# Every inverse norm of a hybrid decoder layer as one power on GpSimd, in place of a shift and three Newton steps on VectorE

## The chip, the cores and the metric

The kernel runs on one core of a Trainium2 chip. The metric is device time in microseconds (us), as the median of several executions. The core has five engines that run their own instruction queues in order: TensorE (PE, with its weight loads shown as PEld), VectorE (DVE), ScalarE (ACT), GpSimd (POOL) and SyncE (SP, which issues the DMAs here). An instruction that waits for a semaphore holds up all that stands behind it in the queue of its own engine.

## The reference, cut to what matters

The layer is: RMS norm of the input, one wide projection, two mixers (sparse attention, and a gated linear recurrence, HGRN2), an output projection with residual, a second RMS norm and a SwiGLU FFN. What the change touches is every place where a mean of squares is turned into its inverse root:

```
def rms_norm(x, g):
    y = xf * lax.rsqrt(jnp.mean(xf * xf, axis=-1, keepdims=True) + RMS_EPS)
    return y * g
h  = rms_norm(x, norm_mix[l])                      # 1024 tokens
q  = rms_norm(q.reshape(B, T, H, dh), q_norm[l])   # 8 heads a token
kc = rms_norm(compress(kc_raw, ...), k_norm[l, 0]) # 63 compressed keys, 2 groups
ks, kw = rms_norm(ks, ...), rms_norm(kw, ...)      # 2 groups a token each
o  = rms_norm(o, o_gain) * silu(hg)                # 4 HGRN heads
h  = rms_norm(x, norm_ffn[l])                      # 1024 tokens again
```

## The kernel before, in words

Tokens lie on the 128 partitions, in NT = 8 tiles of 128. Matmuls of full precision are made of three passes of split operands (lines 118 to 120, "mm3"): ACT writes the high part of an operand (line 111 or 114) and DVE the rest (line 112 or 115). The kernel is written in program order, and a scheduler in the tile framework sorts the instructions into the queue of each engine, so that the place of one in its queue can change when others are added or removed.

The stages, with the span's microseconds: the projection's first two blocks (0 to 80), in which the squares of the input rows are summed on ACT (line 262) and rsx, one inverse norm for each of 8 token tiles, is made (line 264); four HGRN heads (80 to 270), each with seven levels of a recurrence and then an output norm o_rs (lines 417 to 430); the queries, the compressed keys (norm rs), the norm rs_q of all queries (128 x 64) and four batches of keys (norm k_rs, lines 637 to 651) up to 395; the attention units from 395 to 740, with tiles of the output projection between them; a passage to the FFN (740 to 776); and the FFN to the end.

The function rsqrt (line 122) is called 19 times: once for rsx, four times for o_rs, once each for rs and rs_q, four times for k_rs, and eight times for n_rs, in norm_stats (line 239). Each call is v = mean + eps (line 125, a tile named rs_v), a shift (126), a subtraction from a constant (127), and three times a square, a product and a step (129, 130, 131), all on DVE: twelve instructions.

What follows a norm: in an HGRN head o_rs is multiplied by rsx (line 421), scales the head's output out of PSUM (424), which is gated (426) and transposed by PE (429); next stand on PE the first products of the next head (358). In the keys' stage k_rs scales kraw (647), then gain, cast and rest (648 to 650), and PE transposes (657). In the attention stage nsa_out (line 733) sums the squares of a finished token tile on ACT (242), takes n_rs, scales the tile on ACT (745), and multiplies by the gain on POOL (746) for tiles 0 to 6; tile 7 is scaled by one DVE instruction (743). POOL scales each head's weights in the same stage (850), with values that PE then transposes (861). In the passage PE transposes tiles and differences of tiles (724), and ACT and DVE write them as split operands (727, 728); POOL makes two of the differences of a tile (988, 989).

Of the kernel before, what the change touches and what calls it, by code (L numbers as in the profile page):

```python
# [8 lines left out]
F32 = mybir.dt.float32  # L9
F32R = mybir.dt.float32r  # L10
BF16 = mybir.dt.bfloat16
I32 = mybir.dt.int32
U8 = mybir.dt.uint8
AF = mybir.ActivationFunctionType
OP = mybir.AluOpType
# [3 lines left out]
P = 128  # L19
# [29 lines left out]
def hybrid_layer(ctx: ExitStack, tc: tile.TileContext, x, x_t, par, w_in, k_norm, pos_k, pos_v,  # L49
                 ck_w1, ck_w2, cv_w1, cv_w2, w_out, norm_ffn, w_gu, w_down, cst, hmask, out):  # L50
    nc = tc.nc
    V, A, G, PE = nc.vector, nc.scalar, nc.gpsimd, nc.tensor

    const = ctx.enter_context(tc.tile_pool(name="const", bufs=1))
    small = ctx.enter_context(tc.tile_pool(name="small", bufs=2))
# [65 lines left out]

    def rsqrt(y, ss, n, scale, eps, parts=P):
        v = small.tile([P, 64], F32, name="rs_v", tag="rs_v")[:parts, :n]
        t = small.tile([P, 64], F32, name="rs_t", tag="rs_t")[:parts, :n]
        V.tensor_scalar(v, ss, scale, eps, op0=OP.mult, op1=OP.add)
        V.tensor_scalar(t.bitcast(I32), v.bitcast(I32), 1, None, op0=OP.logical_shift_right)
        V.tensor_scalar(y.bitcast(I32), t.bitcast(I32), -1, 0x5F3759DF, op0=OP.mult, op1=OP.add)
        for _ in range(3):
            V.tensor_tensor(t, y, y, op=OP.mult)
            V.scalar_tensor_tensor(t, t, -0.5, v, op0=OP.mult, op1=OP.mult)  # L130
            V.scalar_tensor_tensor(y, t, 1.5, y, op0=OP.add, op1=OP.mult)


    ident = const.tile([P, P], F32, name="ident")
    make_identity(nc, ident)
    identb = const.tile([P, P], BF16, name="identb")
    V.tensor_copy(identb, ident)
    par_t = const.tile([P, 18], F32, name="par_t")
    gains = const.tile([P, 24], F32, name="gains")
    lb_a = const.tile([P, 4], F32, name="lb_a")  # L140
# [98 lines left out]
    def norm_stats(src, junk):  # L239
        ss = small.tile([P, 1], F32, name="n_ss", tag="n_ss")  # L240
        rs = small.tile([P, 1], F32, name="n_rs", tag="n_rs", bufs=NT)
        A.activation(junk, src, AF.Square, accum_out=ss)
        rsqrt(rs, ss, 1, 1.0 / D, EPS)
        return rs
# [5 lines left out]
    with tc.tile_pool(name="p0", bufs=1) as p0:  # L250
# [8 lines left out]
        def x_stats(t):  # L259
            xn = p0.tile([P, D], F32, name="xn", tag="xn", bufs=2)  # L260
            nc.sync.dma_start(xn, x[0, t * P:(t + 1) * P, :])
            A.activation(xn, xn, AF.Square, accum_out=ssx[:, t:t + 1])
            if t == NT - 1:
                rsqrt(rsx, ssx, NT, 1.0 / D, EPS)
                V.tensor_scalar(rsh, rsx, 0.5, None, op0=OP.mult)
# [85 lines left out]
    def hgrn_head(h, hp, fp, qp, kp):  # L351
# [65 lines left out]
        for k in range(2):  # L417
            A.activation(kp[:, 512 * k:512 * (k + 1)], so[k], AF.Square)
        V.tensor_reduce(ss, kp.rearrange("p (c t) -> p c t", c=NT), axis=AX.X, op=OP.add)
        rsqrt(rs, ss, NT, 1.0 / P, 4 * EPS)  # L420
        V.tensor_tensor(rs, rs, rsx, op=OP.mult)
        for k in range(2):
# [875 lines left out]
```

## Time and profile before

| what | us |
|---|---|
| median of 3 executions | 1403.97 (1402.77 to 1405.27) |
| profiled execution | 1403.17 |
| span of its instructions | 1401.3 |
| PE busy | 1369.5 (98%) |
| DVE busy | 1049.3 (75%), 1893 instructions |
| ACT busy | 596.0 (43%) |
| POOL busy | 393.8 (28%), 341 instructions |

The profile gives one execution. Busy time of PE contains the latency of pipelined matmuls, so that a busy PE may still have gaps of some tenths of a microsecond. In a timeline a row gives start and length in us, the engine, the line, what it writes and reads, and in brackets the idle time before it with what ended that. The granted clock of PE was 0.996 of full speed over the span.

### The profile page before, as it was taken

Reading aid. Unit: us, or ns where it says so; the run is one execution under the profiler, and the core shown is the slowest. Engines: PE = TensorE matmul, PEld = TensorE weight load, DVE = VectorE, ACT = ScalarE, POOL = GpSimd, SP = SyncE. Lnnn points to the kernel's source line nnn. Section 1 sums busy time; section 2 is a strip of 40 time slices with the busy share of each in tenths; the row PEclk is TensorE's granted clock in tenths of the full one; section 3 lists DMA queues with packets and bytes.
Section 4 is the critical chain, followed back from the end, with each engine's and each line's share of the span. In section 5 each row is a group of like instructions: output and inputs, shape, how many; then the busy total and the mean of one; then the engine's idle time right before and its main releaser. Section 6 shows DMA issues by size and latency. Waiting matters only on the chain.

```text
span 1401.3 us, 19716 instructions
## 1 busy us (share of the span) xinstructions
PE 1369.5 (98%) x7092; PEld 1129.2 (81%) x7092; DVE 1049.3 (75%) x1893; ACT 596.0 (43%) x1153; POOL 393.8 (28%) x341
## 2 busy tenths in 40 slices
PE   9999999999999999999998999999999999999998
PEld 7888888989977777787776888888888888887787
DVE  5317888626688888789877888888888887589864
ACT  7323333323447666566664433333333333444332
POOL 0001111011045442443436433233232230158500
PEclk9999999999999999999999999999999999999999
DMA  9411110111220001000003333333333328987431
GB/s 336 116 45 31 31 31 28 54 31 46 89 93 1 1 1 61 31 16 31 16 23 98 95 102 97 113 98 113 113 107 99 111 98 285 330 308 270 162 107 54
DMA packets 108769, 135.72 MB, mean 97 GB/s; under 512 B 6112, under 2 KB 63872, under 8 KB 108672
## 3 DMA queue, kind: packets, MB, share of 16 engines
q1 hardware_dynamic: 108672, 134.46, 28.7%
q8 instruction: 56, 0.92, 0.3%
q14 instruction: 41, 0.34, 0.1%
HBM read 105.87 MB, written 28.57 MB: 96 GB/s over the span
## 4 chain that ended last, share of the span: by engine, by line
PE 83%; DVE 12%; ACT 2%; issue 2%; POOL 1%; ACTq 0%; POOLq 0%; DVEq 0%
PE bank L118 9%; PE bank L119 9%; PE bank L120 9%; PE a L118 8%; PE a L119 8%; PE a L120 8%; PE ps_t L119 4%; PE ps_t L118 4%; PE ps_t L120 4%; PE ps_t L861 3%; DVE wop L112 2%; PE a L865 2%; PE a L866 2%; PE ps_t L375 1%; PE ps_s L839 1%
## 5 line engine op out<-in xcount | busy, mean ns | idle before, releaser
L850 POOL TENSOR_SCALAR pbig<-pbig,den,gates 128x640 f32<-128x640 f32 (+7 forms) x128 | 103.5, 812 | 165.5 <-DVE den L849 145.6
L111 ACT ACTIVATE wop<-rpage 128x512 fp32r<-128x512 f32 x132 | 82.7, 630 | 157.8 <-PE bank L120 70.7
L112 DVE TENSOR_TENSOR wop<-rpage,wop 128x512 fp32r<-128x512 f32 x132 | 101.0, 767 | 14.8 <-ACT wop L111 12.6
L864 DVE TENSOR_TENSOR ph<-ps_t,ph 128x512 fp32r<-128x512 f32 x126 | 84.4, 684 | 18.4 <-ACT ph L863 17.4
L863 ACT ACTIVATE ph<-ps_t 128x512 fp32r<-128x512 f32 x126 | 72.6, 595 | 48.2 <-PE ps_t L861 38.5
L381 POOL TENSOR_TENSOR kp<-kp,fp 128x256 f32<-128x256 f32 x28 | 20.3, 724 | 232.3 <-PE bank L358 180.7
L861 PE MATMUL ps_t<-ident,pbig 128*128 128x128 f32 x504 | 78.4, 275 | 2.1 <-POOL pbig L850 2.1
L112 DVE TENSOR_TENSOR wop<-act_a,wop 128x512 fp32r<-128x512 f32 x48 | 47.6, 991 | 32.0 <-ACT wop L111 31.9
L1012 POOL TENSOR_TENSOR tmp<-tmp,rpage 128x512 f32<-128x512 f32 x21 | 31.2, 1487 | 138.9 <-DVE wop L112 138.9
L861 PEld LDWEIGHTS ps_t<-ident,pbig 128*128 128x128 f32 x504 | 60.8, 141 | 11.7 <-POOL pbig L850 3.2
L112 DVE TENSOR_TENSOR wlo<-wraw,whi 128x1024 fp32r<-128x1024 f32 (+2 forms) x27 | 32.0, 1188 | 46.0 <-PE a L120 19.3
L848 ACT ACTIVATE pbig<-ps_s,nm 128x640 f32<-128x640 f32 (+3 forms) x64 | 55.9, 875 | 24.1 <-DVE nm L847 19.0
L119 PE MATMUL bank<-wop 128*128 128x512 f32 x165 | 65.0, 394 | 0.0
L120 PE MATMUL bank<-wop 128*128 128x512 f32 x165 | 64.9, 393 | 0.0
L111 ACT ACTIVATE wop<-act_a 128x512 fp32r<-128x512 f32 x48 | 30.3, 631 | 81.2 <-PE bank L120 56.4
L118 PE MATMUL bank<-wop 128*128 128x512 f32 x165 | 64.8, 393 | 0.0
L847 DVE TENSOR_REDUCE nm<-ps_s 128x1 f32<-128x640 f32 (+3 forms) x64 | 58.1, 914 | 4.7 <-PE ps_s L842 3.1
L865 PE MATMUL a<-ph,kv 128*128 128x512 f32 x132 | 58.6, 444 | 2.1 <-ACT ph L863 1.3
L866 PE MATMUL a<-ph,kv 128*128 128x512 f32 x132 | 57.3, 434 | 2.8 <-DVE ph L864 2.3
L972 POOL TENSOR_TENSOR tmp<-rpage 128x512 f32<-128x512 f32 x20 | 27.4, 1369 | 115.7 <-DMA rpage<-in_w_gate_up_dram 115.7
L112 DVE TENSOR_TENSOR wop<-tmp,wop 128x512 fp32r<-128x512 f32 x42 | 43.6, 1039 | 20.6 <-ACT wop L111 19.2
L111 ACT ACTIVATE wop<-tmp 128x512 fp32r<-128x512 f32 x42 | 26.6, 633 | 70.2 <-POOL tmp L1012 37.5
(458 smaller groups left out, 4454.5 us busy)
## 6 DMA issues: line engine op xcount, KB each, us to landing
rpage<-in_w_gate_up_dram SPq DMA_DIRECT2D x86, 256.0 KB, 3.1
raws<-in_w_down_dram SPq DMA_DIRECT2D x35, 512.0 KB, 7.2
act_a<-act_d SPq DMA_DIRECT2D x12, 1024.0 KB, 6.2
act_d<-as SPq DMA_DIRECT2D x33, 256.0 KB, 2.2
act_e<-act_d SPq DMA_DIRECT2D x6, 1024.0 KB, 7.6
act_d<-tmp SPq DMA_DIRECT2D x22, 256.0 KB, 2.2
act_d<-th SPq DMA_DIRECT2D x22, 256.0 KB, 2.1
xn<-in_x_dram SPq DMA_DIRECT2D x8, 512.0 KB, 5.5
```

Of the source, the lines that this page charges most:

```text
L111: A.activation(hi, src, AF.Copy)
L112: V.tensor_tensor(lo, src, hi.bitcast(F32), op=OP.subtract)
L118: PE.matmul(o, ah, bh, start=first, stop=False, skip_group_check=chained)
L119: PE.matmul(o, ah, bl, start=False, stop=False, skip_group_check=chained)
L120: PE.matmul(o, al, bh, start=False, stop=last, skip_group_check=chained)
L847: V.tensor_reduce(nm, sv, axis=AX.XY, op=OP.max, negate=True)
L850: G.tensor_scalar(pp, pp, den, gates[:, qb, h * 3 + 1 + b:h * 3 + 2 + b], op0=OP.mult, op1=OP.mult)
L861: PE.transpose(pt[:, r * P:(r + 1) * P], wts[r][:, c0:c0 + P], ident)
L863: A.activation(ph[:, 0], pt, AF.Copy)
L864: V.tensor_tensor(ph[:, 1], pt, ph[:, 0].bitcast(F32), op=OP.subtract)
L865: PE.matmul(o, vst[b][:, kb, g, :], ph[:, 0], start=b == 0 and kb == kb0, stop=False)
L866: PE.matmul(o, vst[b][:, kb, g, :], ph[:, 1], start=False, stop=False)
```

## The change

The shift, the subtraction and the nine Newton instructions of rsqrt are gone; v stays on DVE, and one GpSimd instruction raises it to the power -0.5, elementwise, with a constant tile of -0.5 as its second operand. That tile is set once, by a DVE memset at the program's start. Lines behind this function carry numbers that are lower by four after the change (421 becomes 417).

```
     def rsqrt(y, ss, n, scale, eps, parts=P):
         v = small.tile([P, 64], F32, name="rs_v", tag="rs_v")[:parts, :n]
-        t = small.tile([P, 64], F32, name="rs_t", tag="rs_t")[:parts, :n]
         V.tensor_scalar(v, ss, scale, eps, op0=OP.mult, op1=OP.add)
-        V.tensor_scalar(t.bitcast(I32), v.bitcast(I32), 1, None, op0=OP.logical_shift_right)
-        V.tensor_scalar(y.bitcast(I32), t.bitcast(I32), -1, 0x5F3759DF, op0=OP.mult, op1=OP.add)
-        for _ in range(3):
-            V.tensor_tensor(t, y, y, op=OP.mult)
-            V.scalar_tensor_tensor(t, t, -0.5, v, op0=OP.mult, op1=OP.mult)
-            V.scalar_tensor_tensor(y, t, 1.5, y, op0=OP.add, op1=OP.mult)
+        G.tensor_tensor(y, v, mhalf[:parts, :n], op=OP.pow)
...
+    mhalf = const.tile([P, 64], F32, name="mhalf")
+    V.memset(mhalf, -0.5)
```

The change moves instructions in the queues. On DVE, at the end of the first HGRN head, the last Newton steps stood among the next head's work (fp and kp, lines 455 to 459), before o_rs (421), the scaling (424) and the gating (426):

```order
L129 TENSOR_TENSOR rs_t<-o_rs 128x8
L130 SCALAR_TENSOR_TENSOR rs_t<-rs_t,rs_v 128x8
L131 SCALAR_TENSOR_TENSOR o_rs<-rs_t,o_rs 128x8
L129 TENSOR_TENSOR rs_t<-o_rs 128x8
L457 TENSOR_SCALAR kp<-fp 128x512
L130 SCALAR_TENSOR_TENSOR rs_t<-rs_t,rs_v 128x8
L458 TENSOR_SCALAR kp<-kp,lb_a 128x512
L131 SCALAR_TENSOR_TENSOR o_rs<-rs_t,o_rs 128x8
L459 TENSOR_SCALAR fp<-fp,lb_a,lb_b 128x512
L421 TENSOR_TENSOR o_rs<-o_rs,rsx 128x8
L424 TENSOR_TENSOR qp<-bank,o_rs 128x512 x2
L426 TENSOR_TENSOR qp<-qp,gmix 128x512 x2
```

Now, on DVE at the same place:

```order
L415 TENSOR_REDUCE o_ss<-kp 128x8
L124 TENSOR_SCALAR rs_v<-o_ss 128x8
L417 TENSOR_TENSOR o_rs<-o_rs,rsx 128x8
L420 TENSOR_TENSOR qp<-bank,o_rs 128x512 x2
L422 TENSOR_TENSOR qp<-qp,gmix 128x512 x2
L451 TENSOR_TENSOR fp<-a_1129,kv_88 128x512
L453 TENSOR_SCALAR kp<-fp 128x512
L454 TENSOR_SCALAR kp<-kp,lb_a 128x512
```

The product with rsx stands right behind v, and the next head's work behind the gating. On PE, before, the head's last transposes (429) stood in two lots of four behind 34 projection matmuls (118 to 120) counted from the last product of the head's output (414):

```order
L118 MATMUL a_1179<-hT_h,whi 128x512
L119 MATMUL a_1179<-hT_l,whi 128x512
L429 MATMUL bank<-ident,qp 128x128 x4
L120 MATMUL a_1179<-hT_h,wlo 128x512
L429 MATMUL bank<-ident,qp 128x128 x4
L358 MATMUL bank<-qp,kp 128x128 x4
```

Now, on PE, they are one lot of eight behind 20 of these matmuls:

```order
L118 MATMUL a_1159<-hT_h,whi 128x512
L119 MATMUL a_1159<-hT_l,whi 128x512
L120 MATMUL a_1159<-hT_h,wlo 128x512
L425 MATMUL bank<-ident,qp 128x128 x8
L118 MATMUL a_1159<-hT_h,whi 128x512
L119 MATMUL a_1159<-hT_l,whi 128x512
```

So the transposes stand 14 matmuls earlier in the first head; it is 14 in the second, 10 and two half-length ones in the third, and 15 half-length ones in the fourth, where they stay in two lots. On POOL, before, in the first attention unit that norms a token tile (775 are the next queries, 850 the scaling of weights, 746 the product with the gain, 813 the compressed weights):

```order
L775 TENSOR_TENSOR rpage<-qtok,rs_q 128x1024
L850 TENSOR_SCALAR pbig<-pbig,den,gates 128x768 x4
L746 TENSOR_TENSOR x_3322<-x_3322,g_bc 128x1024
L850 TENSOR_SCALAR pbig<-pbig,den,gates 128x640 x2
L813 TENSOR_TENSOR pbig<-pbig,c_den 128x512
```

Now, on POOL at the same place:

```order
L771 TENSOR_TENSOR rpage<-qtok,rs_q 128x1024
L125 TENSOR_TENSOR n_rs<-rs_v,mhalf 128x1
L846 TENSOR_SCALAR pbig<-pbig,den,gates 128x768
L742 TENSOR_TENSOR x_3214<-x_3214,g_bc 128x1024
L846 TENSOR_SCALAR pbig<-pbig,den,gates 128x768 x3
L846 TENSOR_SCALAR pbig<-pbig,den,gates 128x640 x2
L809 TENSOR_TENSOR pbig<-pbig,c_den 128x512
```

The product with the gain has moved in between the four scalings of one unit; on ACT the scaling of the tile (745) moves forward with it, ahead of three of the unit's four exponentials (848). On DVE, before, in the passage, tile 7's Newton steps alternated with the evacuations (728) until its scaling (743):

```order
L728 TENSOR_TENSOR opB<-bank,opB 128x4x128
L129 TENSOR_TENSOR rs_t<-n_rs 128x1
L728 TENSOR_TENSOR opA<-bank,opA 128x4x128
L130 SCALAR_TENSOR_TENSOR rs_t<-rs_t,rs_v 128x1
L728 TENSOR_TENSOR opC<-bank,opC 128x4x128
L131 SCALAR_TENSOR_TENSOR n_rs<-rs_t,n_rs 128x1
L112 TENSOR_TENSOR wop<-rpage,wop 128x512
L743 SCALAR_TENSOR_TENSOR x_3322<-x_3322,n_rs,rpage 128x1024
```

Now, on DVE at the same place:

```order
L124 TENSOR_SCALAR rs_v<-n_ss 128x1
L724 TENSOR_TENSOR opA<-bank,opA 128x4x128
L724 TENSOR_TENSOR opB<-bank,opB 128x4x128 x4
L739 SCALAR_TENSOR_TENSOR x_3214<-x_3214,n_rs,rpage 128x1024
L724 TENSOR_TENSOR opB<-bank,opB 128x4x128 x2
L724 TENSOR_TENSOR opA<-bank,opA 128x4x128
L112 TENSOR_TENSOR wop<-rpage,wop 128x512
```

The scaling of tile 7 stands five evacuations behind v, where it stood nine of them, eleven steps of the inverse root and a split behind, and four evacuations ahead of where it was; on POOL the differences 988 and 989 of the last tile now stand ahead of two products of the FFN's first block (1012, 1015) that they stood behind.

## Rows read from the trace of the kernel before

**Rows 1.** Page, part 1: busy us, share of the span, instructions of each engine.

```profile
PE 1369.5 (98%) x7092; PEld 1129.2 (81%) x7092; DVE 1049.3 (75%) x1893; ACT 596.0 (43%) x1153; POOL 393.8 (28%) x341
```

**Rows 2.** Busy time by stretch: from:to, length, then engines PE, PEld, DVE, ACT, POOL.

```profile
580.00:740.00 160.00, 154.63 (x871) 119.81 (x870) 131.69 (x295) 101.95 (x198) 63.02 (x52) 1.00 0.07 26
740.00:776.00 36.00, 30.16 (x163) 24.01 (x162) 27.98 (x47) 19.70 (x37) 26.84 (x19) 0.95 0.31 88
780.00:1280.00 500.00, 499.51 (x2204) 413.30 (x2203) 407.01 (x510) 172.32 (x285) 157.39 (x106) 1.00 0.47 156
```

**Rows 3.** Groups by line and shape, DVE: busy us, mean ns, idle before.

```profile
L130 DVE SCALAR_TENSOR_TENSOR rs_t<-rs_t,rs_v 128x1 f32<-128x1 f32 x24 | 7.0, 293 | 0.3
L130 DVE SCALAR_TENSOR_TENSOR rs_t<-rs_t,rs_v 128x8 f32<-128x8 f32 x27 | 4.5, 165 | 0.7
```

**Rows 4.** Timeline of the first HGRN head's end, DVE and PE: start, length, instruction.

```profile
148.00 0.17 DVE L125 TENSOR_SCALAR rs_v<-o_ss 128x8 f32<-128x8 f32 x1
151.78 0.16 DVE L421 TENSOR_TENSOR o_rs<-o_rs,rsx 128x8 f32<-128x8 f32 x1
153.17 1.28 DVE L426 TENSOR_TENSOR qp<-qp,gmix 128x512 f32<-128x512 f32 x2
153.91 0.66 PE L429 MATMUL bank<-ident,qp 128*128 128x128 f32 x4 [0.15 <-DVE qp L426]
```

**Rows 5.** Groups by line and shape, POOL: busy us, mean ns, idle before.

```profile
L381 POOL TENSOR_TENSOR kp<-kp,fp 128x256 f32<-128x256 f32 x28 | 20.3, 724 | 232.3 <-PE bank L358 180.7 <-DVE fp L383 51.5
L612 POOL TENSOR_TENSOR jq<-qtok 128x512 f32<-128x512 f32 x8 | 9.9, 1235 | 69.6 <-ACT qtok L435 56.2 <-DVE rs_t L130 13.4
```

**Rows 6.** Timeline of the last batch of keys, DVE, POOL and PE.

```profile
385.98 0.16 DVE L125 TENSOR_SCALAR rs_v<-k_ss 128x8 f32<-128x8 f32 x1
386.59 1.75 DVE L129 TENSOR_TENSOR rs_t<-k_rs 128x8 f32<-128x8 f32 x1
389.98 0.69 DVE L647 TENSOR_TENSOR kraw<-kraw,k_rs 128x512 f32<-128x512 f32 x1
...
386.42 1.90 POOL L775 TENSOR_TENSOR rpage<-qtok,rs_q 128x1024 f32<-128x1024 f32 x1 [2.23 <-PE bank L120]
...
393.20 1.06 PE L657 MATMUL ps_t<-ident,kd 128*128 128x128 f32 x8 [1.42 <-DVE kd L650]
```

**Rows 7.** Waits of PE, 580 to 740 (total, times, longest); then DVE's timeline.

```profile
PE a L866 <- DVE ph L864: 2.3, 6, 0.6
...
590.43 0.83 DVE L130 SCALAR_TENSOR_TENSOR rs_t<-rs_t,rs_v 128x1 f32<-128x1 f32 x1
```

**Rows 8.** Waits of PE, 740 to 776; then DVE's timeline.

```profile
PE a L120 <- DVE wop L112: 1.7, 2, 1.3
PE bank L724 <- DVE opA L728: 1.1, 2, 0.9
PE bank L724 <- POOL d L988: 1.1, 1, 1.1
PE bank L724 <- DVE n_rs L131: 0.6, 1, 0.6
PE bank L724 <- POOL d L989: 0.6, 1, 0.6
...
749.56 0.15 DVE L125 TENSOR_SCALAR rs_v<-n_ss 128x1 f32<-128x1 f32 x1 [0.34 <-ACT rpage L242]
...
759.56 2.30 DVE L743 SCALAR_TENSOR_TENSOR x<-x,n_rs,rpage 128x1024 f32<-128x1024 f32 x1
```

**Rows 9.** Timelines and, for rs_q, the rows of tile rs_v: who uses early norms.

```profile
35.30 0.17 DVE L125 TENSOR_SCALAR rs_v<-ssx 128x8 f32<-128x8 f32 x1 [0.86 <-ACT xn L262]
...
45.15 0.69 ACT L310 ACTIVATE th<-a,rsh 128x512 f32<-128x512 f32 x1
...
L125 DVE TENSOR_SCALAR rs_v<-ssq x1: 189/189/189, 334.9 to 334.9; 128x64 f32<-128x64 f32 x1
...
382.30 1.90 POOL L775 TENSOR_TENSOR rpage<-qtok,rs_q 128x1024 f32<-128x1024 f32 x1 [48.59 <-DVE wlo L112]
```

## The prediction, made before the changed kernel was run

> **What bounds the kernel now.** I read the busy line of the page first: PE is busy for 98% of the span, DVE for 75%, POOL for 28% [rows 1]. The reader is to see that only PE's gaps can be won, whatever DVE is relieved of. Then the stretches: in the FFN, 780 to 1280, PE is busy for 499.51 of 500 us, so nothing is to be won there, and its 2204 matmuls come at 500 / 2204 = 0.227 us each, the price of one place on PE [rows 2]. In the attention stretch with norms, 580 to 740, 160 - 154.63 = 5.4 us are idle, and in the passage, 740 to 776, 36 - 30.16 = 5.8 us [rows 2]. Last the waits of PE and the timelines at the places where a norm is made [rows 4, 6 to 8]. A Newton step on DVE costs 0.165 us for eight columns, but 0.29 us in the mean for one column [rows 3], though it does less work: some of these steps are held up. One took 0.83 us in the first tile's norm [rows 7], and one of eight columns 1.75 us while a product of 1.90 us ran on POOL [rows 6].
>
> **What is removed, and what is added.** 19 calls lose eleven DVE steps each, 209 instructions; 19 powers come to POOL, and one memset to DVE. At 0.165 us or more that is 209 x 0.165 = 34 us or more of DVE time, nearly all beside a busy PE. What counts is the delay from v to the norm at four kinds of places.
>
> **The price of a power.** No row shows one. Its floor is a POOL product of as many columns: from 724 ns at 256 columns and 1235 at 512 the slope is 2.0 ns a column and the rest 213 ns, so 0.23 us for eight columns [rows 5]. For a ceiling I take the eleven steps that it replaces, each as a POOL instruction at that floor: 11 x 0.23 = 2.5 us. The ends are far apart. [...] Of it I count 0.2 us as fixed, as in these rows, and 0.075 us a column: 0.3 us for one column and 5 us for 64. I call the price of eight columns p.
>
> The Trainium skill, GPSIMD Engine Reference, Engine selection, says that an elementwise operation with two inputs is about twice as slow on GpSimd as on VectorE, which speaks against moving one. The trace agrees for products of 128 x 512: 1.24 us on POOL [rows 5] against 0.69 on DVE [rows 6]. By that rule alone p would be 2 x 0.165 = 0.33 us, and the sum below would be some 2.2 us better; whether it holds for a power no row shows, and I don't use it.
>
> **HGRN heads, four norms o_rs: +1.8 us.** Before, v ends at 148.17, line 421 starts at 151.78, and the first half of 426 ends at 153.17 + 0.64 = 153.81; PE transposes at 153.91, after 0.15 us idle [rows 4]. So a handing-over costs about 0.1 us, an estimate from these rows. With the power, 421 can start at 148.17 + 0.1 + p + 0.1 = 149.17, which is 2.6 us earlier, and the transposes at 151.3. But the new order brings PE there 14 x 0.227 = 3.2 us earlier: at 153.91 - 0.15 - 3.2 = 150.6. It waits 0.7 us where it waited 0.15, and as the eight transposes now stand in one lot, about 0.2 us more for the second half: +0.75. The second head is moved alike: +0.75. In the third, 10 matmuls and two halves are gained (2.5 us) and another DVE instruction fills the wait: +0.1. In the fourth 15 half-length ones (1.7 us) stand against about 1.5 us of data: +0.2. Projection matmuls that stood ahead of the transposes now stand behind them, ahead of the next head's first products, whose operands come later on DVE; they are the cover of that. The bounds are -0.3 at p = 0.23 and +8 at p = 2.5, as two to three of four waits grow with p.
>
> **Keys, four norms k_rs: -1.0 us.** Only the last batch has a wait of PE: 1.42 us for 650 [rows 6]. Its v ends at 386.14 and 647 starts at 389.98, with the long step of 1.75 us between [rows 6]. With the power ahead of that product in POOL's queue, k_rs is there at 386.14 + 0.2 + 0.8 = 387.1; but then POOL starts its 1.90 us product, and 647, which reads two tiles from SBUF as the held-up step did, may be held up by it until 389.0. I count 1.0 us, with bounds from -1.42 (all of the wait) to +0.7 (p at its ceiling).
>
> **Attention, seven tiles n_rs from 580 to 740: -1.5 us.** Six waits of PE for 864 on DVE are 2.3 us [rows 7]; five of them follow a held-up Newton step, as the one at 590.43. These go. Against that, POOL's product with the gain now stands between the scalings of one unit, and ACT's scaling of the tile ahead of three of its four exponentials; the weights are needed only a unit later, which covers POOL's part, but ACT's part can show. I count 0.8 us of the 2.3 back. The bounds are -4 (of the 5.4 us idle) and +4, some 0.6 us a tile.
>
> **The passage, tile 7: -4.0 us.** From v at 749.56 to the scaling at 759.56 there are 10 us, of which the eleven steps with their hold-ups are some 4.4; the scaling itself takes 2.30 [rows 8]. In the new order it stands behind five evacuations of about 0.65 us, so it starts near 749.7 + 3.3 = 753, and the power, 0.3 us plus the rest of POOL's differences ahead of it, fits beside these. PE's waits here are 1.7 for the split behind 743, 1.1 for opA, 0.6 for a step of the norm, and 1.1 + 0.6 for POOL's last differences [rows 8]: 5.1 us in all. The last two go, as 988 now stands ahead and its input comes early; so does the wait for the split. Against that the 2.30 us of the scaling now delay three evacuations, for which I keep 1.1 us of waiting: 5.1 - 1.1 = 4.0. The bounds are -5.8 (all idle time) and 0.
>
> **Costed at nothing.** rsx: v at 35.30 and the first reader of rsh at 45.15 [rows 9], so 9.4 us of cover for a power, one small step and two handings-over; DVE stands behind that power with four splits of weights, which PE needs later still. Beyond about 9 us PE would lose what is over. rs_q: v at 334.9 and the first reader at 382.30 [rows 9], 47 us of cover for 64 columns, which cost 5 us by the price above; what is queued behind it on POOL is the next power, for keys. rs of the compressed keys: a power in place of eleven steps, while PE runs the queries' projection. The memset: one instruction, while PE waits for the first loads.
>
> **The sum.** +1.8 - 1.0 - 1.5 - 4.0 = -4.7 us. On the profiled execution, 1403.17 us (a span of 1401.3 and 1.9 around it), that gives 1398.5. The median of the runs lies 0.8 us higher, at 1403.97, and to it I apply the change: 1399.3 us.
>
> **Rivals.** *No change that can be measured (chance 0.22).* A change under 0.2%, 2.8 us, can't be told from none here. For it speaks that PE is at 98% and that the scheduler's new order trades waits: if the scaling among the evacuations costs the passage all but 1 us and the tiles gain nothing, the sum is +1.8 - 1.0 - 1.0 = -0.2, which is 1403.8 us. Against it speaks that the passage's waits name the norm and what stands behind it.
>
> *Slower, as the power is slow (0.26).* The place is the end of each HGRN head, where the transposes have moved up by 3.2 us on PE and DVE stands still behind v. The price there grows by about 3.7 us for each us of p, and by about 1 us in the last batch of keys. From p = 0.8 + 4.7 / 4.7 = 1.8 us on, the change is slower. At p = 2.5 the heads cost +8.1 and the keys +0.7, the rest stays: 8.1 + 0.7 - 1.5 - 4.0 = +3.3, so 1407.3 us. Against it: the floor is eight times lower than this p. For it: no row shows a power, and if it is worked out lane by lane it could be far above my ceiling.
>
> *A larger gain (0.08).* p at 0.33, nothing lost in the tiles, and the whole passage: 0 - 1.4 - 3 - 5.8 = -10.2, so 1393.8 us.
>
> **How the numbers follow.** The forecast has 0.44; its own range is 1397 to 1402. Faster by over 0.2%, below 1401.2: most of the forecast (0.42) and the larger gain (0.08), 0.50. Within 0.2%: 0.22 and the forecast's edge, 0.24. Slower: 0.26. The range of 8 in 10 reaches down to 1393.5, the larger gain, and up to 1409, past the slow power at my ceiling; what is left out is above all a power worked out lane by lane.
>
> **What would show it.** POOL's rows for the power: near 0.8 us at eight columns for my sum, over 1.8 for the slower case. DVE: 1893 - 208 = 1685 instructions, and at least 34 us less busy. PE's waits for 426 at the four transposes: about 0.7 us in two of them; at 657, about 0.4. The held-up steps near 590 and their waits should be gone, with no larger ones for ACT in their place. The scaling of tile 7 should start some 4 to 6 us earlier than 759.56, less what came before, and the wait for 988 be gone. Wrong would be: a wait at the heads that eats the passage's gain, or evacuations that wait for the scaling as long as the splits did.

## The result, and the profile after

The changed kernel takes 1418.24 us (median of 4 executions, 1417.34 to 1419.38); before took 1403.37 (4 executions beside it, 1401.64 to 1405.27; the 1403.97 ahead of the prediction is the median of three of these). The ratio is 1.0109, 95% interval 1.0096 to 1.0121: 14.9 us slower. The forecast was 4.7 us faster, and its wide range ended at 1409. The profiled execution took 1419.38 us with a span of 1417.6, against 1403.17 and 1401.3.

The first part of the page after, in the columns of [rows 1]:

```profile
PE 1374.7 (97%) x7092; PEld 1130.0 (80%) x7092; DVE 1022.6 (72%) x1685; ACT 596.6 (42%) x1153; POOL 425.3 (30%) x360
```

DVE is 26.7 us less busy with 208 instructions fewer, where the prediction had at least 34: the steps alone covered 33.6 us of its busy time in before's trace, and DVE's other instructions cover some 7 us more after. POOL is 31.5 us busier with 19 instructions more. The groups by line and shape on POOL (busy us, mean ns of one, idle before) give the price that [rows 5] could only bound:

```profile
L125 POOL TENSOR_TENSOR rs_q<-rs_v,mhalf 128x64 f32<-128x64 f32 x1 | 10.5, 10549 | 1.0 <-DVE rs_v L124 1.0
...
L125 POOL TENSOR_TENSOR o_rs<-rs_v,mhalf 128x8 f32<-128x8 f32 x4 | 6.6, 1641 | 36.6 <-DVE rs_v L124 36.6
...
L125 POOL TENSOR_TENSOR k_rs<-rs_v,mhalf 128x8 f32<-128x8 f32 x4 | 6.5, 1636 | 23.6 <-DVE rs_v L124 23.6
...
L125 POOL TENSOR_TENSOR n_rs<-rs_v,mhalf 128x1 f32<-128x1 f32 x8 | 4.4, 554 | 42.6 <-DVE rs_v L124 42.6
```

Eight columns cost 1.64 us, twice the 0.8 assumed, and about what the eleven steps took on DVE (11 x 0.165 = 1.8 us [rows 3]). One column costs 0.55 us, less than its steps (0.29 us for one of them in the mean). Only the 64 columns of rs_q cost far more: 10.5 us, against 2.4 for the eleven steps in before's trace. By the rule from the Trainium skill that the prediction weighed (GPSIMD Engine Reference, Engine selection) it would have been 0.33; a power does not follow it.

In the first head's end (timelines of POOL, DVE and PE: start, length, instruction, idle before) the power is followed by the product with rsx, scaling, gating and transposes, as in [rows 4]:

```profile
148.51 1.65 POOL L125 TENSOR_TENSOR o_rs<-rs_v,mhalf 128x8 f32<-128x8 f32 x1 [9.15 <-DVE rs_v L124]
...
150.20 0.17 DVE L417 TENSOR_TENSOR o_rs<-o_rs,rsx 128x8 f32<-128x8 f32 x1 [1.76 <-POOL o_rs L125]
...
152.41 1.26 PE L425 MATMUL bank<-ident,qp 128*128 128x128 f32 x8 [1.55 <-DVE qp L422]
```

The product with rsx starts at 150.20, still 1.6 us earlier than before (151.78). But PE now stands at the transposes 14 products earlier and waits 1.55 us, where it waited 0.15. PE's waits over all four heads, 100 to 275 us (total, times, longest), were 0.5 us for this before:

```profile
PE bank L425 <- DVE qp L422: 5.6, 4, 1.7
```

In the passage (736 to 792) the waits of [rows 8] for 988 and 989 are gone, as forecast, and others stand in their place:

```profile
PE bank L120 <- DVE wop L112: 3.2, 1, 3.2
PE bank L720 <- DVE opB L724: 2.5, 1, 2.5
PE bank L720 <- DVE opA L724: 2.2, 2, 1.3
```

The timelines of DVE, POOL and PE show them:

```profile
765.70 1.98 DVE L739 SCALAR_TENSOR_TENSOR x<-x,n_rs,rpage 128x1024 f32<-128x1024 f32 x1 [0.58 <-DMA rpage<-in_norm_ffn_dram]
...
785.92 0.68 DVE L112 TENSOR_TENSOR wop<-s,wop 128x512 fp32r<-128x512 f32 x1
...
776.08 1.27 POOL L968 TENSOR_TENSOR s<-rpage 128x512 f32<-128x512 f32 x1 [5.65 <-PE bank L720]
...
768.42 1.01 PE L720 MATMUL bank<-ident,d 128*128 128x128 f32 x6 [2.54 <-DVE opB L724]
...
786.66 0.50 PE L120 MATMUL bank<-opB,wop 128*128 128x512 f32 x1 [3.19 <-DVE wop L112]
```

The scaling of tile 7 (739) starts 4.2 us behind v (761.55), the last 0.58 of them a wait for the load of its gain; before it started 10.0 us behind v, and the prediction had 3.4. It stands among the evacuations, and PE waits 2.54 us for the one behind it. The first FFN sum s (968) waits on POOL for a buffer that PE still reads, until 776.08 (758.98 in before's timeline; 11.5 us of the difference come from earlier stages, by the table below); its split on DVE (785.92) stands behind all evacuations, and PE waits 3.19 us for that.

By stretch, in the columns of [rows 2], the tiles have 160 - 152.26 = 7.7 us idle where they had 5.4, and the FFN is as full as it was:

```profile
580.00:740.00 160.00, 152.26 (x860) 117.47 (x859) 121.67 (x218) 100.15 (x197) 70.89 (x62) 1.00 0.06 22
...
790.00:1290.00 500.00, 499.51 (x2201) 413.25 (x2200) 407.20 (x512) 171.53 (x285) 154.01 (x105) 1.00 0.46 154
```

The delay of one and the same instruction against before, worked out from the starts in the traces (us), is the account for all runs. Lines have before's numbers, x1 to x10 are the runs below, and in brackets stands the instruction's start in before. A column is one profiled execution, and holds what PE's clock did in that one.

| instruction (time before) | after | x1 | x2 | x3 | x4 | x5 | x7 | x10 |
|---|---|---|---|---|---|---|---|---|
| head 1, line 358 (116) | 0.2 | 0.0 | -0.5 | 0.2 | 0.3 | 0.6 | 0.5 | -0.5 |
| first 657 (355) | 5.8 | 0.0 | 5.3 | 0.4 | 0.2 | 0.5 | 1.0 | -0.6 |
| last batch 657 (393) | 5.5 | -1.6 | 5.3 | 0.1 | 0.2 | 0.5 | 1.0 | -0.6 |
| third unit, 790 (428) | 7.1 | -1.6 | 5.3 | 1.7 | 1.8 | 0.5 | 2.6 | 0.9 |
| line 865 (585) | 7.2 | -2.4 | 5.4 | 2.1 | 2.0 | 0.9 | 3.3 | 0.1 |
| last 865 (734) | 11.5 | 1.6 | 5.2 | 2.1 | 6.3 | 0.8 | 3.0 | 4.4 |
| first 1013 (779) | 14.3 | 6.7 | 5.1 | 1.9 | 9.5 | 4.9 | 2.5 | 5.1 |
| eleventh 1013 (964) | 15.4 | 7.7 | 5.0 | 1.9 | 10.6 | 6.1 | 2.9 | 5.3 |

After: heads +5.6, keys -0.3, early attention +1.6, tiles +4.4, passage with the first FFN blocks +3.9, and 0.9 behind that.

### The profile page after: what moved, and what is told of

The parts are those of the page before. It is cut to its first block, busy times and chain, and to the rows that moved or that the text cites. A ratio compares the mean times of both kernels' runs of the same rounds, so it can differ in the third digit from the quotient of the medians.

```text
span 1417.6 us, 19551 instructions
## 1 busy us (share of the span) xinstructions
PE 1374.7 (97%) x7092; PEld 1130.0 (80%) x7092; DVE 1022.6 (72%) x1685; ACT 596.6 (42%) x1153; POOL 425.3 (30%) x360
## 4 chain that ended last, share of the span: by engine, by line
PE 83%; DVE 10%; ACT 3%; issue 2%; POOL 1%; DMA 1%; ACTq 0%; SPq 0%; DVEq 0%; POOLq 0%
PE bank L118 9%; PE bank L120 9%; PE bank L119 9%; PE a L120 9%; PE a L118 9%; PE a L119 9%; PE ps_t L119 4%; PE ps_t L118 4%; PE ps_t L120 4%; PE ps_t L857 3%; PE a L861 2%; DVE wop L112 2%; PE a L862 2%; PE ps_t L371 1%; PE ps_s L835 1%
## 5 line engine op out<-in xcount | busy, mean ns | idle before, releaser
L112 DVE TENSOR_TENSOR wop<-rpage,wop 128x512 fp32r<-128x512 f32 x132 | 104.1, 792 | 16.2 <-ACT wop L111 14.0
```

Of the source, the lines that this page charges most:

```text
L112: V.tensor_tensor(lo, src, hi.bitcast(F32), op=OP.subtract)
```

## The experiments

Three theories. Duration: the power itself, 1.64 us on a chain that PE waits for. Order: the scheduler counts a power as short and moves other instructions, and the new order costs, whatever stands in the power's place. Place: neither alone, but a chain of about the old length met earlier by PE.

**x1, a product in place of the power.** Every queue's order is that of the changed kernel.

```
-        V.tensor_scalar(v, ss, scale, eps, op0=OP.mult, op1=OP.add)
-        G.tensor_tensor(y, v, mhalf[:parts, :n], op=OP.pow)
+        V.tensor_scalar(v, ss, 1e-6 * scale, 0.5, op0=OP.mult, op1=OP.add)
+        G.tensor_tensor(y, v, mhalf[:parts, :n], op=OP.mult)
...
-    V.memset(mhalf, -0.5)
+    V.memset(mhalf, 1.0)
```

> The order of every engine is that of the changed kernel; only the operation differs: each power is a product of the same two tiles, and the value under the root is 0.5 plus a millionth of the mean square, so that it takes no root and its output is not the reference's. If the power's own duration (1.64 us at 8 columns, 0.55 at one) costs the 15 us, the time falls back to about the kernel before, 1402 to 1405: heads +0.5 us against before instead of +5.6, tiles and passage within 1. If the order does, only the heads give back their share (about 5 us by 3.7 us for each us of the operation) and tiles and passage keep their +8: 1412 to 1414.

Measured: 1411.86 us, ratio 1.0060 (1.0048 to 1.0073), so 8.7 us slower than before and 6.4 faster than after. The product of 8 columns takes 0.20 us and PE's wait in the heads falls from 5.6 to 0.3; the passage's waits stay to a tenth. The groups on POOL, then the waits of PE from 100 to 275, then from 736 to 792:

```profile
L125 POOL TENSOR_TENSOR o_rs<-rs_v,mhalf 128x8 f32<-128x8 f32 x4 | 0.8, 204 | 36.6 <-DVE rs_v L124 36.6
```

```profile
PE bank L425 <- DVE qp L422: 0.3, 1, 0.3
```

```profile
PE bank L120 <- DVE wop L112: 3.2, 1, 3.2
PE bank L720 <- DVE opB L724: 2.5, 1, 2.5
PE bank L720 <- DVE opA L724: 2.2, 2, 1.3
```

So the heads' loss needs the duration (0.0 in the table against +5.6), and the keys would gain 1.6 us with a short operation. Tiles (+3.9) and passage (+6.1) lose without any power: that is the order. Of the passage's +6.1, though, a part is PE's clock in this execution. By stretch for x1, then for before (the granted clock, as a share of full speed, is the number behind POOL's):

```profile
740.00:800.00 60.00, 51.62 (x242) 39.94 (x241) 46.83 (x62) 26.39 (x49) 36.59 (x26) 0.91 0.29 84
...
740.00:800.00 60.00, 54.16 (x269) 43.88 (x268) 49.97 (x79) 28.16 (x51) 35.58 (x25) 0.97 0.32 93
```

The lower clock is worth up to (0.97 - 0.91) x 60 = 3.6 us, less where PE waits anyway. After, with the same order, had 0.97 like before and lost 3.9 us here, so the loss does not hang on the clock. Neither theory's number was met by its own reasons alone: the order theory's 1412 to 1414 comes close (0.1 us below its edge), but the heads lose nothing here and the keys gain, which it did not count.

**x2, x3, x4: one kind of place each.** The power where the condition holds, Newton's steps elsewhere.

```
+        if n == 8 and scale == 1.0 / P:
+            G.tensor_tensor(y, v, mhalf[:parts, :n], op=OP.pow)
+            return
...
```

That is x2; x3 has `scale == 1.0 / DH or n == NT and scale == 1.0 / D`, x4 `n == 1`.

> The power only for the four HGRN norms of 128x8, Newton's steps everywhere else. If the cost is local to where a power waits, this kernel is about 5.6 us slower than before (1409) and loses nothing after 400 us. If the order that the heads leave behind shifts the later stages as well, it is 10 us or more slower.

> The power only for the norms off the norm-to-product chain: rsx, the compressed keys, rs_q (10.5 us on GpSimd) and the keys' four of 128x8. Local costs: -0.3 us in the keys and +1.6 in the early attention, about 1405. If rs_q's 10.5 us and the keys' powers hold GpSimd where nothing waits, no change (1403.5); the forecast on record had -1.0 here.

> The power only for the eight one-column norms of the attention tiles and the passage. Local costs: tiles +4.4 and passage +3.8, so about 8 us slower (1411 to 1412), with no delay before 580 us. If those delays came from the state that the heads and keys left, it is within 2 us of before; the forecast on record had -5.5 here.

Measured: x2 1408.94 us, ratio 1.0038 (1.0024 to 1.0052), +5.8; x3 1403.43, 1.0005 (0.9996 to 1.0014), +0.3; x4 1412.20, 1.0069 (1.0056 to 1.0082), +9.1. (The us are differences of medians; worked out from the ratios, they would be up to 0.9 us more or less, here and below.) Their sum is 15.2, against 14.9 for all at once: between these three kinds of places the costs are local and add up. x3's trace has the +1.6 of the early attention, and so has x4's, with queue orders there like before's, while x2's does not. It is PE's clock. By stretch for x3:

```profile
420.00:440.00 20.00, 18.08 (x116) 15.38 (x115) 14.79 (x44) 12.38 (x38) 10.36 (x16) 0.91 0.01 1
426.00:432.00 6.00, 6.00 (x34) 5.09 (x34) 3.12 (x11) 3.32 (x12) 2.20 (x4) 0.83 0.02 4
```

And for before and x2, in the same stretch:

```profile
420.00:440.00 20.00, 18.07 (x125) 15.28 (x123) 16.30 (x46) 13.64 (x40) 10.20 (x16) 1.00 0.01 2
...
420.00:440.00 20.00, 18.39 (x124) 15.29 (x122) 16.06 (x51) 14.53 (x45) 11.91 (x20) 1.00 0.00 1
```

It fell after a wait of PE that every run has here (1.4 us for line 850 in before). (1 - 0.91) x 20 = 1.8 us is about the delay. Of the fourteen profiled executions five have the fall (after, x3, x4, x7, x10) and all have the wait. PE's queue is the same in x3 as in before, and the same in after as in x1, and of each pair one has the fall. So in these traces the term goes with one execution or another, not with the order; whether the change makes such falls more frequent is not shown. The profiled spans differ by 16.3 and the medians by 14.9.

**x5, x10: tile 7 alone, tiles 0 to 6 alone.** The power where `t == NT - 1`, or `t < NT - 1`, in nsa_out.

> The power for tile 7's norm alone, Newton's steps for the other sixteen. The order up to the passage is that of before; in the passage 18 matmuls, 18 of ScalarE's steps and two of GpSimd's stand elsewhere. By the order theory the passage loses what it lost with all eight powers: +3.2 us up to the first sums and +1.1 behind them, 1406.5 to 1408. By the forecast on record (the power ends the chain 4 us earlier) 1399.5.

> The power for the norms of tiles 0 to 6 alone. Its order in the passage is that of before. If tile 7 and the other tiles add up, +9.1 less tile 7's +4.9: 1407.5, all of it between 580 and 750 us. By the forecast on record (it had the tiles at -1.5) 1402.

Measured: x5 1408.22 us, ratio 1.0032 (1.0020 to 1.0044), +4.9; x10 1407.54, 1.0033 (1.0022 to 1.0044), +4.3. Together 9.2, as x4. (x5's expectation speaks of the other sixteen norms; it is eighteen.) In x5 nothing but the passage differs, and one norm of one column, whose power takes 0.57 us, costs 4.9 us. The waits of PE there are those of after:

```profile
PE bank L120 <- DVE wop L112: 3.2, 1, 3.2
PE bank L729 <- DVE opB L733: 2.5, 1, 2.5
PE bank L729 <- DVE opA L733: 2.4, 3, 1.3
```

From 740 to 800 the granted clock was 0.91 in x5 and 0.97 in before, up to another (0.97 - 0.91) x 60 = 3.6 us, as in x1: in this trace part of the loss is the clock. After itself had 0.97 and lost 3.9 all the same.

**x6, the split of s first.** x5, with the first FFN sum split right where it is made in the program.

```
     s1s = [gate_up_s1(0, nxt[0][0])]
+    ready[id(s1s[0])] = wring.tile([P, 2, 512], F32R, name="wop", tag="w")
+    split(ready[id(s1s[0])][:, 0], ready[id(s1s[0])][:, 1], s1s[0])
```

product() then takes the split tile from `ready`.

> As the run with tile 7's power alone, but the first feed-forward sum s is split into its two halves ahead of the last pair's evacuations instead of behind them. If the 3.2 us for which TensorE waits for that split (which stands behind nine evacuations on VectorE) are the passage's loss, the time comes back to 1403 to 1404.5. If the loss is the late sum itself (GpSimd's sum waits 5.6 us for a buffer that TensorE still reads), it stays at 1406.5 to 1408.

Measured: 1406.56 us, ratio 1.0021 (1.0012 to 1.0029), +3.2, at the lower edge of the second theory's range. The waits of PE from 736 to 792, and the stretch:

```profile
PE bank L734 <- DVE opB L738: 3.1, 2, 2.5
PE bank L734 <- DVE opA L738: 2.4, 3, 1.3
PE bank L118 <- ACT wop L111: 0.5, 2, 0.3
PE bank L120 <- DVE wop L112: 0.4, 1, 0.4
```

```profile
740.00:800.00 60.00, 53.39 (x262) 41.56 (x261) 43.95 (x67) 28.14 (x51) 36.33 (x26) 0.97 0.29 84
```

The 3.2 us for the split fell to 0.4, and the clock is back at 0.97. The edit gives back 1.7 of tile 7's 4.9 us; how much of that is the wait and how much the clock, these two traces do not separate. The waits for the evacuations round the scaling stay.

**x7, the heads' transposes late.** x2, with both scalings and the transposes written as a function that is called in the next head's projection, ahead of its last three products.

```
+        def last():
             for k in range(2):
...
+        tails.append(last)
...
+                if j == hf == 1 and c == LATER and tails:
+                    tails.pop()()
```

> The power for the four HGRN norms as in the run with the heads alone, but the two scalings and the eight transposes behind it are written late in the next head's projection (before its last three products), so that TensorE meets the transposes about where it met them before. If the heads' 5.3 us need both the 1.64 us and the transposes' earlier place, they are gone: 1403 to 1404. If the power's duration costs wherever the transposes stand, about 1408.5 again.

Measured: 1405.78 us, ratio 1.0014 (1.0004 to 1.0023), +2.4 in place of +5.8, and between the expectation's two numbers. In the heads the delay falls from 5.8 (table, less the start) to 0.5, and PE's wait for the gating from 5.6 to 0.3, with the same power of 1.64 us:

```profile
PE bank L444 <- DVE qp L441: 0.3, 2, 0.2
```

```profile
153.68 1.21 PE L444 MATMUL bank<-ident,qp 128*128 128x128 f32 x8
```

The transposes start at 153.68 without a wait (153.91 before). So in the heads the power's length costs where PE is brought to it early, and not with the transposes at about their old place. (In the keys it costs as well: PE's last wait there is 1.1 us with the power and gone with x1's product.) The rest of its +2.4 lies behind the heads: +1.6 by the clock at 420 to 440 (0.91 in its profile too), and some that I have not assigned.

**x8, x11, x12: other small edits, no power.** x8: `for _ in range(4 if n == 1 else 3)`. x11: two steps everywhere (57 instructions fewer in 19 norms; its expectation counts 51 in seventeen). x12: before with x6's edit.

> No power at all: before, with four Newton steps instead of three in the eight one-column norms, 24 VectorE instructions of 0.14 us more. By durations alone at most 0.5 us slower in tiles and passage. By the order theory the tiles' interleaving changes (some 680 of 6974 TensorE rows stand elsewhere) and with it the time, by more than a microsecond in either direction.

> No power: before with two Newton steps instead of three in all seventeen norms, 51 VectorE instructions less. Shorter chains by 0.3 to 0.5 us at each place, so by durations a gain of 1 to 2 us. By the order theory TensorE's order changes in the heads (the transposes move up by some 9 products) and in the tiles, and the sum can come out on either side by 3 us; heads within 1 of before, since the shorter chain and the earlier place go together here.

> Before (no power) with the one edit that mended part of tile 7's loss: the first feed-forward sum split ahead of the last pair's evacuations. In before the sum's split already stands ahead of seven of them, so 0 to 1 us faster, 1402.5 to 1403.5; if it shifts the evacuations behind it, up to 1 us slower.

Measured: x8 1407.29 us, ratio 1.0026 (1.0018 to 1.0035), +3.9; x11 1405.15, 1.0016 (1.0007 to 1.0024), +2.0; x12 1405.93, 1.0013 (1.0005 to 1.0022), +2.7. Each of these moves a few hundred rows or fewer and each loses 2 to 4 us, also the two that shorten or advance a chain. x8's 24 steps of 0.14 us come to 3.4 us of DVE work, beside a PE whose waits for a Newton step were 0.6 us in before's passage [rows 8]; its +3.9 fits the order theory, without showing which row costs. Its profiled execution is its fastest (1403.90, granted clock 1.00 over the span), and in it the tiles, from the row of 585 to that of 734 in the table, lose 3.1 us all the same; falls of the clock that before's trace has, near 560 and 753 us, are missing there and hide them. x12 lies outside both of its expectation's ranges; PE has a wait in its passage (736 to 792) that before has not:

```profile
PE bank L729 <- DVE opC L733: 2.6, 1, 2.6
```

x12 is also the measure for x6. With the sum split first in both, and each taken against its own before, tile 7's power costs about 3.2 - 2.7 = 0.5 us, where it costs 4.9 in x5 without that edit. So what it costs in the passage depends on the order around it, and is no price of the power. No kernel tried is faster than before. Only x3 leaves PE's queue in before's order, and it alone is not slower.

**x9, sixteen columns in the heads.** x2, each power over the eight columns twice.

```
-        rsqrt(rs, ss, NT, 1.0 / P, 4 * EPS)
...
+        rsqrt(rs2.rearrange("p (w n) -> p w n", w=2), ss[:, None, :].broadcast_to([P, 2, NT]), 2 * NT, 1.0 / P, 4 * EPS)
...
```

> The heads-alone kernel with each power taken over 16 columns, the second eight a copy that nobody reads: at 0.159 us a column the power lasts 2.9 us instead of 1.64, and the place of the first two heads' transposes in TensorE's order is that of the heads-alone kernel. If a head loses the power's duration beyond what its products in front cover, the second head's first scan product comes 1.3 us later than with 8 columns (+2.5 against before, by the heads-alone kernel's +1.2) and the heads lose some 10 us in all: 1413. If handover and order cost and not the duration, 1409 as before.

Measured: 1420.16 us, ratio 1.0116 (1.0100 to 1.0131), +17.0 where 10 was expected. The power takes 2.91 us as worked out, and PE waits 2.82 us for the first head's gating (the row at 154.27), about 1.3 us longer than in x2. But the second head's first scan product is delayed by 4.3 us against the start, not by 2.9 (x2's 1.6 and the power's 1.3 more). The group on POOL, then a PE row, then two stretches:

```profile
L127 POOL TENSOR_TENSOR o_rs<-rs_v,mhalf 128x16 f32<-128x16 f32 x4 | 11.6, 2906 | 36.6 <-DVE rs_v L126 36.6
```

```profile
154.27 1.97 PE L437 MATMUL bank<-ident,qp 128*128 128x128 f32 x8 [2.82 <-DVE qp L434]
...
156.47 0.63 PE L119 MATMUL a<-hT_l,whi 128*128 128x512 f32 x1
156.89 0.63 PE L120 MATMUL a<-hT_h,wlo 128*128 128x512 f32 x1
...
157.71 0.40 PE L119 MATMUL a<-hT_l,whi 128*128 128x512 f32 x1
157.94 0.39 PE L120 MATMUL a<-hT_h,wlo 128*128 128x512 f32 x1
```

```profile
148.00:156.00 8.00, 5.18 (x25) 4.22 (x23) 4.25 (x8) 0.57 (x1) 2.92 (x1) 0.89 0.00 1
156.00:164.00 8.00, 8.00 (x38) 6.58 (x36) 5.85 (x10) 3.86 (x6) 0.00 (x0) 0.90 0.24 68
```

Products follow each other at 0.42 us after the wait (156.47, 156.89) and at 0.23 later (157.71, 157.94): the lower of the clock's two levels, 1.2 of 2.4 GHz. In x2, with waits of at most 1.7 us, the clock is 1.00 in both stretches. The clock adds 8 x (0.11 + 0.10) = 1.7 us to this head. The other heads' ends, second to fourth:

```profile
198.00:206.00 8.00, 7.86 (x35) 6.63 (x36) 5.36 (x10) 2.97 (x4) 0.00 (x0) 0.79 0.23 66
236.00:246.00 10.00, 7.20 (x40) 5.72 (x38) 6.02 (x11) 3.58 (x5) 2.42 (x1) 1.00 0.00 0
274.00:282.00 8.00, 5.04 (x41) 4.84 (x40) 4.05 (x7) 1.07 (x2) 2.90 (x1) 0.91 0.00 1
282.00:290.00 8.00, 8.00 (x49) 8.00 (x48) 0.27 (x1) 2.33 (x4) 0.00 (x0) 0.67 0.50 139
```

With 8 x 0.21 in the second and 8 x (0.09 + 0.33) in the fourth, the clock adds 6.7 us in all, and the 10 expected and these 6.7 are about the 17 measured. In the third head PE waits 2.80 us, as in the first, and the clock stays at 1.00.

## Why the prediction was wrong, by its steps

- **The price p: mis-sized.** No run shows the 0.8 us that the sum takes for eight columns; 1.64 were measured; 0.3 for one, 0.55 measured; 5 for 64, 10.5 measured. The split of the price into a fixed 0.2 and 0.075 a column had the right form and half the size: a column costs 0.159 us, where the product's slope was 2.0 ns [rows 5].
- **HGRN heads, +1.8: mechanism right, size off by p.** With p = 1.64 its slope of 3.7 gives 1.8 + 0.84 x 3.7 = 4.9; measured 5.6. The largest miss is the fourth head, about 2.0 by the starts where 0.2 was forecast. Between x1 and after the slope is (5.6 - 0.0) / (1.64 - 0.20) = 3.9 us per us. x7 shows the other half, the transposes' place.
- **Keys, -1.0: right in kind.** Measured -0.3, with PE's wait for the last batch down from 1.42 [rows 6] to 1.1; with a short operation (x1) the whole wait goes, -1.6. PE's wait after, 384 to 400 us:

```profile
PE ps_t L653 <- DVE kd L646: 1.1, 1, 1.1
```

- **Tiles, -1.5: failed.** Measured +4.4, +3.9 with a cheap product. The step counted the waits behind held-up Newton steps as gone. They did shrink: PE's waits for the rest of ph, 2.3 us in [rows 7], are 1.1. But the new order brought others that the step priced at 0.8 us. After, from 580 to 736 (the first was 2.1 us before, the second is new):

```profile
PE ps_s L835 <- ACT pbig L844: 2.4, 6, 1.2
PE a L118 <- DVE rpage L506: 1.7, 2, 1.5
```

  The longest single one is a wait of 1.46 us for the cast of the output projection's operand, which on DVE and POOL looks like this:

```profile
695.40 1.97 DVE L506 CAST rpage<-qtok 128x512 fp32r<-128x512 f32 x1
...
749.71 0.43 DVE L506 CAST rpage<-qtok 128x512 fp32r<-128x512 f32 x1
...
694.73 2.36 POOL L742 TENSOR_TENSOR x<-x,g_bc 128x1024 f32<-128x1024 f32 x1
...
697.43 0.51 PE L118 MATMUL a<-whi,rpage 128*128 128x512 f32 x1 [1.46 <-DVE rpage L506]
```

  The cast takes 0.43 us with POOL idle and 1.97 beside the gain's product, ending 0.3 us after that ends. The Trainium skill, SBUF — State Buffer, Who interferes with whom, says that a cast may take the port pair that DVE shares with GpSimd, and that the one that starts later waits for the whole instruction; these rows agree. With the Newton steps gone, another DVE instruction met the product. The waits sum to 2.2 us more than before; the rest of the 4.4 is not assigned to rows.
- **The passage, -4.0: failed.** The waits that it named did go: 988, 989, the split behind the scaling; and the scaling came nearly as soon behind v as it said (4.2 us, 3.4 forecast). It set against them 1.1 us for evacuations behind the scaling; that wait alone is 2.5. And it did not follow the first FFN sum, which the same reorder sent behind PE's reading of a buffer and its split behind all evacuations: 3.2 us, a wait that the step put at nothing. Measured +3.9; in x5, from one power of 0.57 us, +4.9.
- **Costed at nothing: right.** rsx, rs and rs_q cost nothing that x3 can show (its interval is -0.6 to +2.0 us), though rs_q took 10.5 us. The memset too. The +1.6 of the early attention is the clock, for which the sum had no term.
- **The rivals.** The slower case came true in sign and not in mechanism: p stayed below its break-even of 1.8, and by the forecast's own formula p = 1.64 would give -4.7 + 0.84 x 4.7 = -0.8, about 1403. (Its floor is eleven times below 2.5 us, not eight.) Tiles and passage, 13.8 us from the forecast's terms together, made the result: both steps counted the waits that the new order ends and not those that it begins.

## What to carry to other kernels

Price a change in a scheduled program by what the scheduler moves, place by place: a shorter-looking chain pulls its readers forward in the queues of in-order engines, and these then wait if the chip does not deliver. Count for each moved row which new neighbour it stalls or is stalled by, not only which old waits go; and test with a cheap operation of the same shape, which keeps the order and takes out the duration. Here every kernel that moved PE's order lost about 2 us or more, so a gain of a few microseconds off the critical engine is worth little against a shuffle of it.

## What the runs showed of the hardware

A power on GpSimd costs about 0.40 us and 0.159 us for each column of 128 lanes: 0.554, 1.641, 2.906 and 10.549 us for 1, 8, 16 and 64 columns. That of 63 x 2 took 1.41 us after, beside a split on DVE that had started 0.17 us before it. A product costs 0.204 us at eight columns. TensorE's granted clock fell to the lower level after a wait of 2.82 us in x9's first head, so that this wait cost more than its length, and stayed up after waits of 1.7 (x2). But the length of a wait does not settle it: the clock stayed at 1.00 after 2.80 us in x9's third head and after 2.54 us in after's passage (760 to 780), and after the wait of 1.4 us near 423 it fell in some executions of the same queue order and not in others.
